# First layer's output product: its last 512 weight rows by seven block products instead of a plain product

## The chip, the cores and the metric

The kernel runs on one core of a Trainium2 chip. Times are device microseconds (us) of one launch. One execution of the kernel was also recorded by the hardware profiler. All views below are of that execution; in them times count from the start of its span.

## The reference, cut to what matters

A two-layer encoder works on 512 tokens of width 1024. The first layer mixes tokens by dilated window attention (8 heads of 128), the second by grouped-query attention with axial rotary positions. Each layer also attends over 256 memory rows (4 heads of 128), gates the twelve heads' outputs with a SiLU and multiplies them by an output matrix of 1536 x 1024. That last product, in the first layer, is what the change is about.

```python
for i in range(DEPTH):
    h = rmsnorm(x, norm_g[i])
    mem_h = rmsnorm(mem, mem_norm_g[i])
    ...
    o_mem = memory_attention(q_mem, mem_h, w_mem_kv[i], mem_qn_g[i], mem_kn_g[i])
    y = jnp.concatenate([o_mix, o_mem], axis=-1) * jax.nn.silu(gate)
    x = x + jnp.einsum('bse,ed->bsd', y, w_out[i])
return x
```

Everything is fp32.

## The kernel before, in words

**Products.** An fp32 product is made of three matmuls on operands that are split in two: a rounded copy (the high half) and what the rounding left out (the low half). `mm_early` issues high x high (line 176) and activation low x weight high (line 177), `mm_late` issues activation high x weight low (line 180). A group of twelve 512-wide matmuls is the unit of work. In the group's order all eight of lines 176 and 177 stand first, alternating, and the four of line 180 last.

**Weights.** All weights lie in one array in the order of their use. `PLAN` names the kind of each stretch, `Weights` loads pieces of 0.5 MB with SyncE's queue as buffers come free (`KEEP` sets how many may be alive), copies them to a high half on ScalarE (line 323) and subtracts for the low half on VectorE (line 333). Both halves lie in rings of four. Each group advances the ring.

**Seven products for eight.** `s_chunk` multiplies a 2 x 2 block matrix of activations by a 2 x 2 block matrix of weights with seven block products (Winograd's form of Strassen's scheme). The seven activation operands ("forms": 12, 11, S1, S2, S4, S3, 22) are sums of the four blocks, and the seven weight operands (21, 11, T1, T2, 22, T3, T4) sums of the weight blocks. T1 and T3 are loads that add to a block already loaded; T2 and T4 add one tile to another within SBUF. These adding transfers go through GpSimd's queue (lines 261 and 307; T1 of early stretches, below the index `T1_DMA`, is added by VectorE at line 297). Products that share a term are accumulated in one PSUM bank. `keep` copies a bank out after a product, `add` adds to such copies (lines 411 and 420). With `tail` given, which only the second layer's output product did, form 22 comes ahead of S3, its product in a bank of its own, and the handlers in `tail` carry the sums into the residual.

**Order.** Nothing is left to a scheduler. The program is written as coroutines that a hand-written driver steps: one slot (`drv.tick`) for each group of matmuls. `drv.release(gen, d)` starts the work behind a product after d slots, `yield n` gives up n slots, `drv.late` and `drv.soon` put an instruction at the end or the start of a slot. So the order on each engine is fixed when the program is built, and each engine runs its own in that order. A semaphore wait stops everything behind it on its engine.

**The first layer's end.** `gates` makes, for the four gate blocks of gate group g = 2 (heads 4 to 7 of the attention), the gate times the heads' outputs: line 870 writes y in fp32, line 894 copies it to a high half (ScalarE), line 896 subtracts (VectorE). Heads' outputs go through a tensor in device memory, except that of head 7 (`DIRECT`), the last one computed, which is taken from SBUF. `out_proj` first multiplies the other 1024 rows of the output matrix by `s_chunk` (two weight tiles for each of its products; `tight`, `place`), the sums going to the tiles `acc`, to each of which a transfer adds x (line 1003, GpSimd's queue). Then `out_rest` multiplies y of g = 2 by the remaining 512 rows: per half of the tokens (two blocks of 128) and per half of the columns two groups, eight in all, on two stretches "O1" of the plan with two weight tiles each. Line 806 adds each group's result to `acc`.

**What follows it.** `ev_o` takes each finished block of 128 tokens of x1, the second layer's input: it writes it to device memory (line 1459), makes the sum of squares (`norm_1`, lines 527 and 529), scales it by the norm (`norm_2`, line 534) and transposes it with TensorE (`turn4`, line 540), whose result is copied to a high half (line 164, ScalarE) and subtracted for a low half (line 167, VectorE). The first two blocks ("upper rows") end in `first_t`, the last two ("lower rows") in `diffs_t` and `rest_t`, which make the second layer's forms (lines 600, 601 and 609 among them). Meanwhile `mem_norm(1)`, started 14 slots (`MEM_B`) after line 1469, normalises the memory rows for the second layer (the tiles `m`, line 534 also), and they are transposed by lines 540, 164 and 167 as well, in the slots of the stage that is changed. Behind it come eight groups of `mem_kv`, the second layer's memory keys and values, with squares of heads on ScalarE (line 633) and multiplications on VectorE (line 638).

**The second layer's end** has the same last 512 rows already done by `s_chunk(512, YL, ..., K=2, tail=...)`: `prep_l` (line 954) makes the forms, and its `put` hands the two halves to the driver:

```python
def put(k, src):
    t = m4(F32R, "yl" + k)
    drv.late(lambda: A.copy(t[:, 0:512], src))
    drv.soon(lambda: V.tensor_tensor(t[:, 512:1024], src, t[:, 0:512].bitcast(F32), ALU.subtract))
```

Of the kernel before, what the change touches and what calls it, by code (L numbers as in the profile page):

```python
# [10 lines left out]
F32 = mybir.dt.float32  # L11
# [25 lines left out]

PLAN = ["W2"] + ["T2"] * 2 + ["W1", "W2s"] + ["W2" if c.isdigit() else "W1" for c in A_ORDER[1:]] + ["W2"] + ["O1"] * 2 + ["T2b"] * 2 + ["W1bs", "W2c"] + ["W1b"] * 4 + ["W2b", "W1o"]

SEQ = [1, 2, 0] + list(range(3, len(PLAN)))  # L40
T4_AT = {4: 4}
T1_DMA = 17
SUM_AT = {"T1": 7, "T3": 10}
# [88 lines left out]
def trunk_kernel(ctx: ExitStack, tc: tile.TileContext, x, mem, wall, norm_g, mem_norm_g, gcol,  # L132
# [257 lines left out]
    def s_chunk(n, act, ev, tokens=True, pre=None, half=False, soon=False, tight=False, place=None, pairs=False, K=4, tail=None):  # L390
# [35 lines left out]
        def mid(u, b):  # L426
            t = snap["21", u] = s2(name="sn")
            tail[1](u, t, b)
            yield 1

        if tail:
            after = after[:5] + ((mid,),)
        for i, (a, s, fresh) in enumerate(PRODUCTS[:5] + (("22", 2, True), ("S3", 1, False)) if tail else PRODUCTS):
# [4 lines left out]
            for x in range(K // per):  # L438
# [7 lines left out]

                if tail and i == 6:
                    for b, c in ((0, slice(0, 512)), (1, slice(0, 512))):
                        o, ts = bank[s][b][:, c], slice(b * 128, (b + 1) * 128)
                        for k in range(per):  # L450
                            mm_early(o, ah[:, k, ts], wh[:, k, c], al[:, k, ts], wh[:, k, c], False)
                        for k in range(per):
                            mm_late(o, ah[:, k, ts], wo[:, k, c], k == per - 1)
                        while ("21", 1) not in snap:
                            drv.free()
                            drv.tick()
                        tail[2](b, snap["21", b], snap["s5", b], o, c)
                    continue
# [373 lines left out]
    def gates(od, o_done, o_here, direct, forms=False):  # L832
# [121 lines left out]
        def prep_l():  # L954

            def put(k, src):
                t = m4(F32R, "yl" + k)
                drv.late(lambda: A.copy(t[:, 0:512], src))
                drv.soon(lambda: V.tensor_tensor(t[:, 512:1024], src, t[:, 0:512].bitcast(F32), ALU.subtract))
                YL[k] = t.rearrange("p (a k t) -> p a k t", a=2, k=2)  # L960

            while ys[2] is None:
                yield 1
            put("12", ys[2])
            yield 1
            while ys[0] is None:
                yield 1
            put("11", ys[0])
            yield 1
            while ys[1] is None or ys[3] is None:  # L970
                yield 1
            a11, a21, a12, a22 = ys
            s1, s2_ = s2(name="yl"), s2(name="yl")
            V.tensor_tensor(s1, a21, a22, ALU.subtract)
            put("S1", s1)
            yield 1
            V.tensor_tensor(s2_, s1, a11, ALU.subtract)
            put("S2", s2_)
            yield 1
            V.tensor_tensor(a12, a12, s2_, ALU.add)  # L980
            put("S4", a12)
            yield 1
            put("22", a22)
            yield 1
            V.tensor_tensor(a21, a11, a21, ALU.subtract)
            put("S3", a21)

        return gate, prep_y, YW, (prep_l, YL) if forms else ys

    def out_proj(YW, ys, src, evac, tiles, half=False, last=None):  # L990
# [15 lines left out]

        if last:
            prep_l, YL = ys
            drv.spawn(prep_l())
        s_chunk(512, YW, ev, half=half, tight=True, place=place)  # L1010
        if not last:
            out_rest(ys, acc, done, evac)
            return

        def ev_l(q, u, t):
# [6 lines left out]
        def sum_11(u, z, p):  # L1022
# [4 lines left out]
            yield 1  # L1027
            yield from evac(0, u, acc[u])

# [17 lines left out]

        s_chunk(512, YL, ev_l, tight=True, K=2, tail=(sum_kept, sum_21, final, sum_11))

# [392 lines left out]

    gate, prep_y, YW, ys = gates(od, o_done, o_here, DIRECT)
    for c in A_ORDER:
# [345 lines left out]
```

## Time and profile before

| what | value |
|---|---|
| median of 3 runs | 943.03 us (942.79 to 943.77) |
| the profiled execution's own time | 942.18 us |
| span of its profile, first to last instruction | 940.4 us |
| busy: PE / PEld / DVE / ACT / POOL | 99% / 87% / 85% / 74% / 37% |
| lines 176, 177, 180 in the chain that ended last | 25% of the span each |
| bytes moved | 207.15 MB, 220 GB/s on average |

PE is TensorE's matmul side, PEld its weight load, DVE is VectorE, ACT is ScalarE, POOL is GpSimd, SP is SyncE. A row of the list of waits reads: engine, tile, line, "<-" and the engine, tile and line that ended the wait, then its total in us, the count and the longest. A row of a timeline reads: start and duration in us, engine, line, operation, what is written "<-" what is read, the shapes, and the number of equal instructions that the row takes together; brackets behind it give the idle time ahead and what ended it. A row of the windows reads: the stretch, its length, the busy time of PE, PEld, DVE, ACT and POOL with their instructions, the granted clock of TensorE, the share of the DMA engines' time and the GB/s. A row of the DMA issues reads: what is written and read, queue, count, KB each, median us from issue to landing. Matmuls overlap, so a matmul's time in a row is longer than its distance to the next.

### The profile page before, as it was taken

What the parts mean: (1) busy time and instruction counts of PE and PEld (TensorE: products, weight loads), DVE (VectorE), ACT (ScalarE), POOL (GpSimd) and SP (SyncE); (2) the same over time, 40 slices, a digit from 0 to 9 for tenths busy, and PEclk for the clock granted to TensorE, in tenths of its full rate; (3) what the DMA queues carried; (4) which work ended last, traced back from release to release, by engine and by line L of the source; (5) the groups of instructions that cost most, each with busy time, mean ns of one, the idle gap of its engine ahead of it and who ended that gap; (6) DMA issues with size and microseconds to landing.
All of it is one profiled execution on the core that took longest, in us unless ns stands there. A gap on an engine that the chain in (4) does not pass through costs nothing.

```text
span 940.4 us, 16301 instructions
## 1 busy us (share of the span) xinstructions
PE 932.0 (99%) x5500; PEld 819.4 (87%) x5500; DVE 799.6 (85%) x1443; ACT 691.6 (74%) x1720; POOL 348.4 (37%) x494
## 2 busy tenths in 40 slices
PE   8999999999999999999999999999999999999998
PEld 6889888888888888888889998888988999999886
DVE  6998776879888888889788999877998998689978
ACT  7775788677768686867675768537878887789773
POOL 3412425455554545463836111214252440110122
PEclk9999999999999999999999999999999999999999
DMA  9999937869787878696867979979985686785777
GB/s 346 387 259 324 316 93 189 278 133 262 155 251 146 261 155 267 158 268 136 242 177 190 269 202 249 291 239 317 270 201 118 171 240 167 198 225 121 200 159 179
DMA packets 89285, 207.15 MB, mean 220 GB/s; under 512 B 25201, under 2 KB 34417, under 8 KB 89202
## 3 DMA queue, kind: packets, MB, share of 16 engines
q1 hardware_dynamic: 68674, 140.51, 43.5%
q0 software_dynamic: 19520, 63.97, 36.8%
q10 hardware_dynamic: 1008, 1.64, 0.5%
q8 instruction: 43, 0.70, 0.3%
q14 instruction: 40, 0.33, 0.1%
HBM read 158.31 MB, written 11.08 MB: 180 GB/s over the span
## 4 chain that ended last, share of the span: by engine, by line
PE 95%; DVE 2%; ACT 1%; DMA 1%; issue 0%; SPq 0%; DVEq 0%; ACTq 0%
PE pj L177 25%; PE pj L176 25%; PE pj L180 25%; PE qT L645 3%; PE sa L1305 2%; PE oo L1413 2%; PE pt L1392 1%; PE ptb L1619 1%; PE sa L1301 1%; PE xT L540 1%; PE ob L180 1%; PE ob L177 1%; PE ob L176 1%; PE sb L171 1%; PE sb L170 1%; PE sb L172 1%
## 5 line engine op out<-in xcount | busy, mean ns | idle before, releaser
L333 DVE TENSOR_TENSOR wo<-wl,wh 128x1024 fp32r<-128x1024 f32 x258 | 316.3, 1232 | 6.9 <-ACT wh L323 6.7
L323 ACT CAST wh<-wl 128x1024 fp32r<-128x1024 f32 x258 | 272.1, 1061 | 31.0 <-PE pj L177 17.4
L176 PE MATMUL pj<-wh,hS 128*128 128x512 f32 (+1 forms) x416 | 154.4, 380 | 0.0
L177 PE MATMUL pj<-wh,hS 128*128 128x512 f32 (+1 forms) x416 | 149.0, 367 | 0.0
L176 PE MATMUL pj<-wh,h 128*128 128x512 f32 (+1 forms) x312 | 115.3, 378 | 0.0
L177 PE MATMUL pj<-wh,h 128*128 128x512 f32 (+1 forms) x312 | 111.7, 367 | 0.0
L488 POOL TENSOR_TENSOR rstd<-mse,half 128x4 f32<-128x4 f32 (+2 forms) x98 | 103.4, 1056 | 8.2
L180 PE MATMUL pj<-wo,hS 128*128 128x512 f32 (+1 forms) x416 | 99.5, 366 | 0.0
L177 PEld LDWEIGHTS pj<-wh,hS 128*128 128x128 f32 x416 | 78.7, 189 | 11.2
L176 PEld LDWEIGHTS pj<-wh,hS 128*128 128x128 f32 x416 | 78.6, 189 | 11.1 <-DVE sn L420 0.2
L487 POOL TENSOR_SCALAR mse<-hss 128x4 f32<-128x4 f32 (+1 forms) x88 | 47.8, 543 | 101.9 <-ACT junk L633 94.2
L180 PEld LDWEIGHTS pj<-wo,hS 128*128 128x128 f32 x416 | 72.5, 189 | 13.1
L633 ACT ACTIVATE junk<-sn 128x128 f32<-128x128 f32 x264 | 79.4, 311 | 2.7 <-DVE sn L411 2.6
L398 ACT COPY sn<-pj 128x512 f32<-128x512 f32 x122 | 67.1, 588 | 17.8 <-PE pj L180 17.0
L1249 POOL TENSOR_TENSOR ta<-sn,tabs 128x128 f32<-128x128 f32 (+1 forms) x64 | 35.8, 566 | 119.0 <-DVE sn L638 91.8
L180 PE MATMUL pj<-wo,h 128*128 128x512 f32 (+1 forms) x312 | 74.5, 365 | 0.0
L307 POOL DMA_DIRECT2D wl<-wl x34 | 30.2, 897 | 113.3 <-DVE wo L333 73.3
L261 POOL DMA_DIRECT2D wl<-in_wall_dram x40 | 38.0, 966 | 80.4 <-DMA wl<-in_wall_dram 41.0
L177 PEld LDWEIGHTS pj<-wh,h 128*128 128x128 f32 x312 | 59.0, 189 | 8.4
L176 PEld LDWEIGHTS pj<-wh,h 128*128 128x128 f32 x312 | 59.0, 189 | 8.2
L420 DVE TENSOR_TENSOR sn<-pj,sn 128x512 f32<-128x512 f32 x89 | 60.8, 684 | 5.7 <-PE pj L180 5.3
L180 PEld LDWEIGHTS pj<-wo,h 128*128 128x128 f32 x312 | 54.3, 189 | 9.7
(290 smaller groups left out, 2367.2 us busy)
## 6 DMA issues: line engine op xcount, KB each, us to landing
wl<-in_wall_dram SPq DMA_DIRECT2D x224, 512.0 KB, 7.4
wl<-wl POOLq DMA_DIRECT2D x68, 512.0 KB, 5.5
wl<-in_wall_dram POOLq DMA_DIRECT2D x44, 512.0 KB, 8.5
od<-o SPq DMA_DIRECT2D x11, 256.0 KB, 5.4
og<-od SPq DMA_DIRECT2D x10, 256.0 KB, 9.5
x<-in_x_dram SPq DMA_DIRECT2D x4, 512.0 KB, 9.1
v0d<-sn SPq DMA_DIRECT2D x8, 256.0 KB, 8.5
acc<-in_x_dram POOLq DMA_DIRECT2D x8, 256.0 KB, 6.2
```

What stands on the lines that cost most here:

```text
L176: T.matmul(o, a, b, start=start, stop=False, skip_group_check=True)
L177: T.matmul(o, c, d, start=False, stop=False, skip_group_check=True)
L180: T.matmul(o, a, b, start=False, stop=stop, skip_group_check=True)
L261: queue.dma_start(t, wall[d], **how)
L323: A.copy(wh, self.tile[self.items[i]])
L333: V.tensor_tensor(wo, self.tile[key], wh.bitcast(F32), ALU.subtract)
L398: A.copy(t, b)
L420: V.tensor_tensor(t, b, t, ALU.subtract if q == "12" else ALU.add)
L487: G.tensor_scalar(e, ss, EPS, None, ALU.add)
L488: G.tensor_tensor(r, e, half[:, 0:n], ALU.pow)
L633: A.activation(jk, p[:, j * 128:(j + 1) * 128], AF.Square, scale=by, accum_out=ss[:, j:j + 1])
L1249: G.tensor_tensor(ta[:, 0:n], xn[:, 0:n, 0:32], ropeA[:, 0, b, s0:s0 + n], ALU.mult)
```

## The change

The last 512 weight rows of the first layer's output matrix (last in the kernel's order: those of attention heads 4 to 7, gate group g = 2) are no longer multiplied by `out_rest` but by `s_chunk` with K = 2, as in the second layer. Eight groups of twelve matmuls on four weight pieces become seven groups on seven weight tiles, which six loads and four adding steps make: T1 and T3 are loads that add (`T1_DMA` goes from 17 to 16, so that this stretch's T1 is one too), T2 and T4 adds within SBUF. `gates` in the first layer is called with `forms=True`: the high and low halves of y (lines 894 and 896) are not made; `prep_l` makes the seven forms from the fp32 y instead.

`tail` now has a fifth part, and its third may be empty. Empty, as in the first layer, the last product is issued like the others and `fin` adds its bank to the sums kept, both column halves of a lower block at once, and passes them to `ev_o`. In the second layer the last product is still done column half by column half.

`prep_l`'s `put` no longer hands its instructions to the driver: it issues the high half at once, gives up a slot and issues the low half in the next one. That holds for both layers; in the second layer each engine's order of instructions is the same as before.

```diff
-PLAN = ["W2"] + ["T2"] * 2 + ["W1", "W2s"] + ["W2" if c.isdigit() else "W1" for c in A_ORDER[1:]] + ["W2"] + ["O1"] * 2 + ["T2b"] * 2 + ["W1bs", "W2c"] + ["W1b"] * 4 + ["W2b", "W1o"]
+PLAN = ["W2"] + ["T2"] * 2 + ["W1", "W2s"] + ["W2" if c.isdigit() else "W1" for c in A_ORDER[1:]] + ["W2", "W1o"] + ["T2b"] * 2 + ["W1bs", "W2c"] + ["W1b"] * 4 + ["W2b", "W1o"]
...
-T1_DMA = 17
+T1_DMA = 16
...
+        def fin(u, b):
+            t, c = snap["21", u], snap["s5", u]
+            V.tensor_tensor(t, b, t, ALU.add)
+            V.tensor_tensor(c, c, b, ALU.subtract)
+            yield 1
+            yield from tail[4](u, t, c)
+
         if tail:
-            after = after[:5] + ((mid,),)
+            after = after[:5] + ((mid,), (fin,))
...
-                if tail and i == 6:
+                if tail and tail[2] and i == 6:
...
             def put(k, src):
                 t = m4(F32R, "yl" + k)
-                drv.late(lambda: A.copy(t[:, 0:512], src))
-                drv.soon(lambda: V.tensor_tensor(t[:, 512:1024], src, t[:, 0:512].bitcast(F32), ALU.subtract))
+                A.copy(t[:, 0:512], src)
+                yield 1
+                V.tensor_tensor(t[:, 512:1024], src, t[:, 0:512].bitcast(F32), ALU.subtract)
                 YL[k] = t.rearrange("p (a k t) -> p a k t", a=2, k=2)
...
-            put("12", ys[2])
-            yield 1
+            yield from put("12", ys[2])
...
-        if last:
-            prep_l, YL = ys
-            drv.spawn(prep_l())
+        prep_l, YL = ys
+        drv.spawn(prep_l())
         s_chunk(512, YW, ev, half=half, tight=True, place=place)
-        if not last:
-            out_rest(ys, acc, done, evac)
-            return
-
...
-            yield from evac(0, u, acc[u])
+            if last:
+                yield from evac(0, u, acc[u])
...
-        s_chunk(512, YL, ev_l, tight=True, K=2, tail=(sum_kept, sum_21, final, sum_11))
+        s_chunk(512, YL, ev_l, tight=True, K=2, tail=(sum_kept, sum_21, last and final, sum_11, lambda u, *o: evac(1, 2 + u, o)))
...
-    gate, prep_y, YW, ys = gates(od, o_done, o_here, DIRECT)
+    gate, prep_y, YW, ys = gates(od, o_done, o_here, DIRECT, True)
```

In the changed kernel the lines above 428 keep their numbers and those below move by a few: 527, 529, 534, 540, 638 and 870 become 534, 536, 541, 547, 645 and 877. The rows of order below, of the changed kernel, have its own numbers. Line 967 is `put`'s subtraction, lines 980, 982, 984 and 987 make the forms S1, S2, S4 and S3.

The first place is VectorE's order in the stage itself. `wo` are weights' low halves, `m` the memory rows, `act` their low halves after the transposes, `pj` banks of PSUM, `yl` and `sn` tiles of 512 columns. Before:

```order
L896 TENSOR_TENSOR y_6824<-sn_7042,y_6823 128x2x256
L896 TENSOR_TENSOR y_6824<-sn_7002,y_6823 128x2x256
L420 TENSOR_TENSOR acc_7339<-pj_7498,acc_7339 128x512
L420 TENSOR_TENSOR acc_7340<-pj_7499,acc_7340 128x512
L333 TENSOR_TENSOR wo_7535<-wl_7410,wh_7534 128x1024
L806 TENSOR_TENSOR acc_7217<-pj_7557,acc_7217 128x512
L333 TENSOR_TENSOR wo_7574<-wl_7443,wh_7573 128x1024
L534 SCALAR_TENSOR_TENSOR m_7545<-m_7545,rm_73,row_7543 128x512 x2
L806 TENSOR_TENSOR acc_7218<-pj_7578,acc_7218 128x512
L534 SCALAR_TENSOR_TENSOR m_7546<-m_7546,rm_73,row_7543 128x512 x2
L167 TENSOR_TENSOR act_7617<-xT_7619,act_7615 128x4x128
L167 TENSOR_TENSOR act_7618<-xT_7626,act_7616 128x4x128
```

And now, from the first scaling of the memory rows on:

```order
L541 SCALAR_TENSOR_TENSOR m_7539<-m_7539,rm_73,row_7537 128x512 x2
L967 TENSOR_TENSOR ylS1_7578<-yl_7575,ylS1_7578 128x512
L982 TENSOR_TENSOR yl_7576<-yl_7575,sn_6892 128x512
L333 TENSOR_TENSOR wo_7600<-wl_7438,wh_7599 128x1024
L541 SCALAR_TENSOR_TENSOR m_7540<-m_7540,rm_73,row_7537 128x512 x2
L167 TENSOR_TENSOR act_7640<-xT_7642,act_7638 128x4x128
L167 TENSOR_TENSOR act_7641<-xT_7649,act_7639 128x4x128
L967 TENSOR_TENSOR ylS2_7608<-yl_7576,ylS2_7608 128x512
L984 TENSOR_TENSOR sn_7038<-sn_7038,yl_7576 128x512
L333 TENSOR_TENSOR wo_7632<-wl_7298,wh_7631 128x1024
L167 TENSOR_TENSOR act_7640<-xT_7684,act_7638 128x4x128
L167 TENSOR_TENSOR act_7641<-xT_7691,act_7639 128x4x128
```

The additions of a group's result (line 806) are gone. The scalings of the memory rows and their low halves (lines 541 and 167) stand where they stood in the stage, and the forms and their low halves (lines 982, 984 and 967) stand between them: S2's low half right behind the first pair of lines 167, S4's behind the second pair.

The second place is TensorE around the fourth of the seven groups, the product of form S2, now:

```order
L177 MATMUL pj_7612<-wh_7528,ylS1_7578 128x512
L176 MATMUL pj_7613<-wh_7528,ylS1_7578 128x512
L177 MATMUL pj_7613<-wh_7528,ylS1_7578 128x512
L180 MATMUL pj_7612<-wo_7529,ylS1_7578 128x512 x2
L180 MATMUL pj_7613<-wo_7529,ylS1_7578 128x512 x2
L547 MATMUL xT_7642<-ident_68,m_7539 128x128 x4
L547 MATMUL xT_7649<-ident_68,m_7539 128x128 x4
L176 MATMUL pj_7580<-wh_7569,ylS2_7608 128x512
L177 MATMUL pj_7580<-wh_7569,ylS2_7608 128x512
```

The eight transposes that the first pair of lines 167 reads (`xT`) stand directly ahead of the group, and its second matmul (line 177) reads the low half that VectorE makes behind that pair. The transposes themselves have not moved: before, too, they stood behind the third and the fourth group of the stage.

The third place is VectorE where the lower rows of x1 are scaled for the second layer, during the groups of `mem_kv`. Before:

```order
L167 TENSOR_TENSOR h12_7800<-xT_7853,h12_7800 128x4x128
L167 TENSOR_TENSOR h11_7808<-xT_7860,h11_7808 128x4x128
L333 TENSOR_TENSOR wo_7848<-wl_7576,wh_7847 128x1024
L333 TENSOR_TENSOR wo_7851<-wl_7593,wh_7850 128x1024
L534 SCALAR_TENSOR_TENSOR acc_7339<-acc_7339,rstd_7830,row_7132 128x512 x2
L534 SCALAR_TENSOR_TENSOR acc_7340<-acc_7340,rstd_7881,row_7132 128x512 x2
```

And now:

```order
L167 TENSOR_TENSOR h12_7900<-xT_7966,h12_7900 128x4x128
L167 TENSOR_TENSOR h11_7908<-xT_7973,h11_7908 128x4x128
L541 SCALAR_TENSOR_TENSOR sn_7796<-sn_7796,rstd_7878,row_7127 128x512
L541 SCALAR_TENSOR_TENSOR sn_7674<-sn_7674,rstd_7878,row_7127 128x512
L645 TENSOR_TENSOR xn_7999<-pj_7816,rstd_7955 128x512
L333 TENSOR_TENSOR wo_7961<-wl_7765,wh_7960 128x1024
L333 TENSOR_TENSOR wo_7964<-wl_7802,wh_7963 128x1024
L541 SCALAR_TENSOR_TENSOR sn_7829<-sn_7829,rstd_7930,row_7127 128x512
L541 SCALAR_TENSOR_TENSOR sn_7676<-sn_7676,rstd_7930,row_7127 128x512
```

The second scaling of the lower rows has moved behind one head's multiplication and two weights' low halves. On TensorE the upper rows' transposes stood after the first and the second group of `mem_kv` and now stand after the third and the fourth; the lower rows' stood after the fifth and the sixth and now after the sixth and the seventh.

More of the change, by code (lines that the diff above doesn't have):

```diff
@@ L963, in prep_l @@
                 yield 1
-            put("12", ys[2])
-            yield 1
+            yield from put("12", ys[2])
             while ys[0] is None:
                 yield 1
-            put("11", ys[0])
-            yield 1
+            yield from put("11", ys[0])
             while ys[1] is None or ys[3] is None:
@@ L974, in prep_l @@
             V.tensor_tensor(s1, a21, a22, ALU.subtract)
-            put("S1", s1)
-            yield 1
+            yield from put("S1", s1)
             V.tensor_tensor(s2_, s1, a11, ALU.subtract)
-            put("S2", s2_)
-            yield 1
+            yield from put("S2", s2_)
             V.tensor_tensor(a12, a12, s2_, ALU.add)
[L981 to L984, printed above, removed]
+            yield from put("S4", a12)
+            yield from put("22", a22)
             V.tensor_tensor(a21, a11, a21, ALU.subtract)
-            put("S3", a21)
+            yield from put("S3", a21)
         return gate, prep_y, YW, (prep_l, YL) if forms else ys
```

## The prediction

> **What bounds the kernel now.** I read the page's busy times first, then the list of waits of TensorE, then the timelines of TensorE, VectorE and ScalarE around the stage that is changed.
>
> ```profile
> span 940.4 us, 16301 instructions
> PE 932.0 (99%) x5500; PEld 819.4 (87%) x5500; DVE 799.6 (85%) x1443; ACT 691.6 (74%) x1720; POOL 348.4 (37%) x494
> ...
> PE row L1121 <- DMA row<-in_mem_norm_g_dram: 2.2, 1, 2.2
> PE pmt L772 <- DVE pmT L778: 0.7, 1, 0.7
> ```
>
> TensorE (PE) works through the whole span; behind its first wait of 2.2 us no wait is longer than 0.7 us. So a matmul that goes shortens the kernel by its place in the stream, and any new wait of TensorE lengthens it in full. VectorE (DVE), at 85%, is the next engine. I call the eight groups that go G1 to G8, the seven new products P1 to P7, and the eight groups of the second layer's memory keys and values that follow M1 to M8.
>
> ```profile
> 607.25 0.39 PE L176 MATMUL pj<-wh,y 128*128 128x512 f32 x1
> 609.97 0.39 PE L176 MATMUL pj<-wh,y 128*128 128x512 f32 x1
> ...
> 615.41 1.03 PE L540 MATMUL xT<-ident,m 128*128 128x128 f32 x8
> 616.20 0.48 PE L176 MATMUL pj<-wh,y 128*128 128x512 f32 x1
> 616.52 0.40 PE L177 MATMUL pj<-wo,y 128*128 128x512 f32 x1
> ...
> 630.79 0.39 PE L176 MATMUL pj<-wh,act 128*128 128x512 f32 x1
> ```
>
> G1 starts at 607.25, G2 at 609.97, M1 at 630.79. A group of 12 matmuls takes 2.72 us (0.227 each, though a row says 0.39: they overlap). Eight transposes cost 0.79 and slow the next start by about 0.10, so 0.89; 8 x 2.72 + 2 x 0.89 = 23.54 is just 630.79 - 607.25. The stage has no gap.
>
> **The matmuls that go.** Eight groups become seven: **-2.72 us**. Without any wait M1 would start at 628.07. Everything else in the change is on other engines, and costs only what TensorE waits for.
>
> **When VectorE reaches the new work.** Each product uses the low half of its form in its second matmul (line 177), not at the end of a group, so the subtraction at line 967 must be over 0.23 us after the product's start. Its place in VectorE's order stands in the section on the change.
>
> ```profile
> 603.60 1.23 DVE L333 TENSOR_TENSOR wo<-wl,wh 128x1024 fp32r<-128x1024 f32 x1 [1.71 <-ACT wh L323]
> 604.75 0.42 DVE L870 TENSOR_TENSOR sn<-sn,og 128x256 f32<-128x256 f32 x1
> 605.75 0.42 DVE L870 TENSOR_TENSOR sn<-sn,o 128x256 f32<-128x256 f32 x1
> 606.09 1.28 DVE L411 TENSOR_TENSOR acc<-acc 128x512 f32<-128x512 f32 x2
> 607.29 1.29 DVE L896 TENSOR_TENSOR y<-sn,y 128x512 fp32r<-128x512 f32 x2
> 608.50 1.28 DVE L420 TENSOR_TENSOR acc<-pj,acc 128x512 f32<-128x512 f32 x2
> 609.70 1.22 DVE L333 TENSOR_TENSOR wo<-wl,wh 128x1024 fp32r<-128x1024 f32 x1
> 612.56 1.41 DVE L534 SCALAR_TENSOR_TENSOR m<-m,rm,row 128x512 f32<-128x512 f32 x2
> ```
>
> Head 7's multiplications (line 870) are over only at 606.1, 1.2 us before the stage starts, and all forms descend from them. Nothing ahead of them moves, so they stand at 604.75 afterwards too. Back to back a 512-wide operation takes 0.60 us (606.09 to 607.29 for two; 0.69 to its own end), so each has 0.09 of overlap; less that, a weights' low part is 1.14 (1.23) and a scaled one some 0.67 (half of 1.41). From line 411 to the last form's low part the new order has 23, 6 and 4 of these: 13.8 + 6.8 + 2.7 = 23.3 us, so that one ends at 629.5 with no wait at all. P7's second matmul is due at 607.25 + 6 x 2.72 + 1.78 + 0.23 = 625.6. By VectorE's work alone, then, the stage ends 4 us late. The engine's spare time before (0.4 to 2 us here and there) is what the two fewer lines 896, eight lines 806 and TensorE's longer stage had left.
>
> ```profile
> 605.53 1.29 ACT L894 CAST y<-sn 128x512 fp32r<-128x512 f32 x2 [0.66 <-DVE sn L870]
> 616.05 1.08 ACT L164 CAST act<-xT 128x512 fp32r<-128x512 f32 x2 [8.27 <-PE xT L540]
> 616.66 1.29 DVE L167 TENSOR_TENSOR act<-xT,act 128x512 fp32r<-128x512 f32 x2 [0.77 <-ACT act L164]
> 12.64 0.68 DVE L167 TENSOR_TENSOR act<-xT,act 128x512 fp32r<-128x512 f32 x1
> 13.38 0.50 PE L177 MATMUL pj<-wh,act 128*128 128x512 f32 x1 [0.32 <-DVE act L167]
> ```
>
> The last two rows, from the program's start, are a low part that ends at 13.32 and the matmul that waits for it, 0.06 later; I use that for every release. Row by row:
>
> P1: the high half is copied where line 894 stood, over at 606.2. The low part starts at 607.29, ends at 607.98, the matmul goes at 608.04 instead of 607.48: **0.56**. P2: two lines 420 and a weights' part, low part to 610.92, matmul at 610.98 instead of 610.76: **0.22**. P3: the S1 form, a weights' part, two scalings of the memory rows, low part to 614.59, matmul at 614.65 instead of 613.70: **0.95**.
>
> P4 is a loop. Ahead of its low part VectorE's order has the two lines 167, which need ScalarE's copies of the transposes that TensorE does right before P4. From the start of those transposes (615.41 before) the second line 167 ends 2.54 later (617.95), the low part 0.60 after it, the matmul 0.06 after that: 3.20, where it would have come after 0.79 + 0.31 = 1.10. **2.10**, and the same for P5, whose low part stands behind the lines 167 of the second transposes: **2.10**. This does not depend on how loaded VectorE is. P6's low part is 1 us early. P7: from P5's low part on, 3 weights' parts and 8 others put the last one at 632.46, matmul at 632.52 instead of 631.49: **1.03**. Together 6.96, and M1 starts at 635.0, 4.2 after before's 630.79.
>
> For these waits the lower bound is the two loops alone, 4.2 (the rest would go if VectorE were 2 to 3 us ahead, and 4.0 is also its work alone). I take the walk, since its durations all stand in rows.
>
> **The second layer's low parts.** Nothing moves there: line for line the engines' orders are those of before, so the moved put costs 0. The same stage there shows what it needs to be hidden:
>
> ```profile
> 906.32 1.43 DVE L870 TENSOR_TENSOR sn<-sn,o 128x256 f32<-128x256 f32 x4
> 910.53 0.68 DVE L959 TENSOR_TENSOR yl<-sn,yl 128x512 fp32r<-128x512 f32 x1
> 928.46 0.68 DVE L959 TENSOR_TENSOR ylS<-sn,ylS 128x512 fp32r<-128x512 f32 x1
> ...
> 916.40 0.39 PE L176 MATMUL pj<-wh,yl 128*128 128x512 f32 x1
> 932.86 0.39 PE L176 MATMUL pj<-wh,ylS 128*128 128x512 f32 x1
> ```
>
> There the multiplications start 10.1 us before the first product and the low parts are 5.2 (first) and 3.7 us (last) early. In the first layer they start 2.5 us before it, 7.6 us later by that clock, and the memory rows' work comes on top.
>
> **What is late next.** x1's upper rows are now transposed after M3 and M4 instead of M1 and M2, the lower ones after M6 and M7 instead of M5 and M6: three groups apart, not four.
>
> ```profile
> 633.52 1.03 PE L540 MATMUL xT<-ident,acc 128*128 128x128 f32 x8
> 646.18 1.03 PE L540 MATMUL xT<-ident,acc 128*128 128x128 f32 x8
> 649.80 1.03 PE L540 MATMUL xT<-ident,acc 128*128 128x128 f32 x8
> ...
> 640.31 1.29 DVE L167 TENSOR_TENSOR h<-xT,h 128x512 fp32r<-128x512 f32 x2 [4.25 <-ACT h L164]
> 643.79 1.41 DVE L534 SCALAR_TENSOR_TENSOR acc<-acc,rstd,row 128x512 f32<-128x512 f32 x2
> 645.65 1.42 DVE L534 SCALAR_TENSOR_TENSOR acc<-acc,rstd,row 128x512 f32<-128x512 f32 x2 [0.46 <-POOL rstd L488]
> ```
>
> Before, the first lower block was normalised at 645.20, 11.7 us after the first transposes began, and was due at 646.18, 12.7 after: 1.0 to spare. One group less leaves it 1.7 late, if the chain (high copies, first copies, squares, weights' copies, then the second pair) is as long; the new order has the squares of four heads ahead and two weights' parts fewer, about even. **1.7**. The second block stands, in the new order, behind one head product and two weights' parts: 0.6 + 2.3 + 1.3 + 0.1 = 4.3 after the first, where TensorE takes 0.89 + 2.72 = 3.6: **0.6**. Bounds: nothing, if the chain shortens by 2.3, and 4 if it lengthens as much. For the second layer's forms behind M8 I add 0.
>
> **Weights and queues.** Four loads become six loads, two loads that add and two adds within SBUF: 3 MB more at 0.5 MB each; and four adds of 0.25 MB carry P1 and P2 into acc, on POOL's queue.
>
> ```profile
> 564.10:607.20 43.10, 43.10 (x214) 36.41 (x213) 40.12 (x63) 31.93 (x52) 6.09 (x7) 1.00 1.00 285
> ...
> wl<-wl POOLq DMA_DIRECT2D x68, 512.0 KB, 5.5
> wl<-in_wall_dram POOLq DMA_DIRECT2D x44, 512.0 KB, 8.5
> ```
>
> The rings are full there already (share 1.00, 285 GB/s): 3 MB are 10.5 us of traffic. T1's add and T2's add follow each other (8.5 + 5.5 us), POOL stands still for the first, and the x adds queue behind it; ScalarE wants T2 at about 606.7. Up to 610.4 a late landing costs nothing, since VectorE takes that tile at 611.4; later it costs one for one. I take 0, bound +3. On SP, x1's rows go out behind P5 to P7 and hold the next weights back some 4 us of a lead of over 15: 0.
>
> **Sum.** -2.72 + 6.96 + 2.3 = **+6.5 us**. The profiled execution took 942.18 (span 940.4 and 1.8 around it), so 948.7; the runs' median, 943.03, lies 0.85 above it: **949.6**.
>
> **Rivals.**
>
> *Hidden* (4%): VectorE gets to the forms 4 us earlier and the loops close, so only the matmuls count: 943.03 - 2.72 = 940.3, faster. For it: the second layer's tail. Against it: line 870 at 604.75, and a loop that starts with transposes no order can hurry. It decides from the point where P4's low part ends before P4's start.
>
> *Loops alone* (14%): P1 to P3 and P7 and the normalisations do not wait: -2.72 + 4.20 = +1.5, 944.5. Against it: 23.3 us of work in the 19.4 from 606.09.
>
> *Late weights* (12%): T2 lands behind 610.4 by 3 us, VectorE stands, all behind it slips: 952.6.
>
> *A slower clock* (5%): TensorE idles 2.1 of 5.6 us twice.
>
> ```profile
> 8.30 0.63 PE L176 MATMUL pj<-wh,act 128*128 128x512 f32 x1
> 14.18 0.39 PE L176 MATMUL pj<-wh,act 128*128 128x512 f32 x1
> ...
> core 0: 940.4 us, clock 1.000
> ```
>
> At the program's start a matmul takes 0.63, later 0.39. If P5 and P6 ran at half pace, 5.4 us more: 955. Against it: a granted clock of 1.000 over the whole span, its short waits included. The Trainium skill (TensorE: Matmul & The Clock Gate, "HAM oscillation — how this bites in real kernels") puts the limit at idle gaps of some 3.4 us. By that rule gaps of 2.1 keep the clock.
>
> The change not doing what it says would leave 96 matmuls; the order shows 84.
>
> **How the numbers follow.** The sum has 65%, the rivals 35%. Below 0.2% (1.9 us), about what a measurement of this kernel can tell from no change, lies *Hidden* on the fast side, and half of *Loops alone* could read as same. The rows I can quote make the waits, so: faster 0.04, same 0.05, slower 0.91. The range runs from the two loops and P7 alone, 944.5 + 1.0 = 945.5, to late weights, 953.
>
> **What would show it.** Right: TensorE waits on line 967 in five products, about 2.1 us each in P4 and P5; M1 near 635; VectorE without a gap from 604 to 629 but for the two loops; two waits on line 541 after M6 and M7; granted clock 1.00. Wrong: P4 and P5 without a wait, a DMA as the releaser of line 323, or a lower clock.

## The result, and the profile after

The changed kernel takes 955.93 us (median of 6 runs, 952.84 to 958.64), the kernel before 943.31 (6 runs, 942.79 to 943.97): a ratio of 1.0133, interval 1.0109 to 1.0157. It is slower by 12.6 us. The forecast was slower, 949.6 in a range of 945.5 to 953.0, so the sign was right and the size about half of what came.

The profiled execution took 958.00, its span is 956.2. The page's head:

```profile
span 956.2 us, 16326 instructions
PE 937.0 (98%) x5488; PEld 821.7 (86%) x5488; DVE 809.5 (85%) x1457; ACT 701.0 (73%) x1734; POOL 354.3 (37%) x502
```

TensorE's rows of the list of waits, without three that stood there before (lines 1119, 779 and 652):

```profile
PE pj L177 <- DVE ylS L967: 5.3, 3, 2.9
PE pj L176 <- DVE sn L420: 2.6, 1, 2.6
...
PE xT L547 <- ACT junk L640: 1.2, 1, 1.2
...
PE pj L177 <- DVE hS L616: 0.7, 1, 0.7
PE pt L1390 <- DVE p L1377: 0.7, 2, 0.5
PE pj L177 <- DVE yl L967: 0.4, 1, 0.4
PE xT L547 <- DVE sn L541: 0.4, 1, 0.4
```

Before, no wait behind the program's start was longer than 0.7. Now 6 us lie on the forms' low halves (line 967) and 5 behind the stage. Without line 1390, which lies ahead of the stage (at 540 us), the waits sum to 10.6; 12 matmuls fewer take 2.7 away; that makes 8, where the span grew by 15.8. The timeline of TensorE in the stage shows a second cost:

```profile
609.49 0.50 PE L177 MATMUL pj<-wh,yl 128*128 128x512 f32 x1 [0.40 <-DVE yl L967]
...
616.09 0.50 PE L177 MATMUL pj<-wh,ylS 128*128 128x512 f32 x1 [0.65 <-DVE ylS L967]
...
618.73 1.03 PE L547 MATMUL xT<-ident,m 128*128 128x128 f32 x8
619.52 0.48 PE L176 MATMUL pj<-wh,ylS 128*128 128x512 f32 x1
622.88 0.50 PE L177 MATMUL pj<-wh,ylS 128*128 128x512 f32 x1 [2.88 <-DVE ylS L967]
...
624.35 0.63 PE L177 MATMUL pj<-wh,ylS 128*128 128x512 f32 x1
624.78 1.91 PE L180 MATMUL pj<-wo,ylS 128*128 128x512 f32 x4
626.49 1.65 PE L547 MATMUL xT<-ident,m 128*128 128x128 f32 x8
627.90 0.48 PE L176 MATMUL pj<-wh,ylS 128*128 128x512 f32 x1
630.14 0.50 PE L177 MATMUL pj<-wh,ylS 128*128 128x512 f32 x1 [1.77 <-DVE ylS L967]
```

P4 and P5 wait for the low halves of S2 and S4, as forecast. But from 624.35 on a matmul takes 0.63 instead of 0.39, and four of line 180 take 1.91 where they took 1.07: TensorE runs at half speed. The windows give the granted clock (the column behind POOL):

```profile
615.00:620.00 5.00, 4.35 (x22) 3.10 (x21) 4.10 (x6) 2.76 (x5) 2.98 (x4) 1.00 1.08 209
620.00:625.00 5.00, 2.12 (x8) 1.79 (x9) 3.63 (x5) 2.88 (x6) 0.00 (x0) 0.93 1.07 298
625.00:630.00 5.00, 3.37 (x13) 2.58 (x12) 1.80 (x3) 3.47 (x7) 0.86 (x1) 0.73 0.65 119
630.00:635.00 5.00, 4.86 (x14) 3.85 (x15) 4.97 (x9) 2.44 (x5) 0.86 (x1) 0.66 0.75 157
```

A clock of 0.93, 0.73 and 0.66 over 5 us each is at most 0.35 + 1.35 + 1.70 = 3.4 us of TensorE's time. In the trace's record of the clock these are two stretches of 3.41 us at half clock, from 624.33 and from 631.16, and a third follows at 678.94, behind the longest wait of the second layer's first products:

```profile
679.00 0.58 PE L176 MATMUL pj<-wh,hS 128*128 128x256 f32 x1 [2.65 <-DVE sn L420]
```

So the executions differ: with a granted clock of 0.998 or 1.000 over the span they took 952.84, 953.97 and 954.44, with 0.994 to 0.996 they took 957.42, 958.00 and 958.64.

The table places the loss by four points of TensorE's timeline: P1's first matmul (607.25 before), M1 (630.79), the second layer's first product (656.13), and the transposes of line 772 in the second layer's memory attention (716.57). Each entry is how much longer the stretch up to that point is than in the profile of before.

| kernel | to P1 | stage | M1 to M8 | second layer's first products | rest | span |
|---|---|---|---|---|---|---|
| changed | 1.45 | 7.58 | 1.97 | 5.00 | -0.21 | 15.8 |
| low halves as before | -0.29 | 3.10 | 2.31 | 5.04 | -0.18 | 10.0 |
| memory rows early | 2.25 | -0.34 | 4.67 | 5.03 | -0.16 | 11.5 |
| T1 by VectorE | 0.02 | 5.36 | 2.32 | 3.60 | -0.15 | 11.2 |
| fin at once | 1.79 | 6.76 | 0.00 | 3.64 | -0.21 | 12.0 |
| three edits | 0.16 | 4.56 | 0.15 | 1.11 | -0.20 | 5.8 |
| GpSimd adds | 2.40 | -0.85 | 6.37 | 5.16 | -0.18 | 12.9 |
| no low halves | 0.20 | 2.01 | 5.34 | 4.95 | -0.14 | 12.4 |
| four edits | 2.78 | -0.79 | 0.00 | 2.55 | -0.19 | 4.4 |
| no low halves, fin at once | 1.03 | -0.09 | 1.92 | 2.57 | -0.15 | 5.3 |
| four edits, chain earlier | 4.12 | -0.56 | 5.51 | 4.28 | -0.21 | 13.1 |

Where the memory rows are early, their 1.78 us of transposes have moved from the second column to the first. In the two kernels of four edits 1.2 of the first column is P1's own wait. The rest of it need not be the change's: the profile of the first probe below, which differs from the kernel before in nothing ahead of P1, lost 2.2 there as well.

### The profile page after: what moved, and what is told of

Read it like the earlier page. It is cut to its first block, busy times and chain, and to the rows that moved or that the text cites. A ratio compares the mean times of both kernels' runs of the same rounds, so it can differ in the third digit from the quotient of the medians.

```text
span 956.2 us, 16326 instructions
## 1 busy us (share of the span) xinstructions
PE 937.0 (98%) x5488; PEld 821.7 (86%) x5488; DVE 809.5 (85%) x1457; ACT 701.0 (73%) x1734; POOL 354.3 (37%) x502
## 4 chain that ended last, share of the span: by engine, by line
PE 83%; DMA 7%; DVE 6%; ACT 3%; issue 1%; SPq 0%; DVEq 0%; POOLq 0%; ACTq 0%
PE pj L177 21%; PE pj L176 21%; PE pj L180 21%; DMA wl<-in_wall_dram 3%; PE qT L652 2%; DVE wo L333 2%; DMA wl<-wl 2%; DMA og<-od 1%; PE ptb L1617 1%; PE sa L1303 1%; PE oo L1411 1%; PE sa L1299 1%; PE pt L1390 1%; PE xT L547 1%; PE ob L180 1%
## 5 line engine op out<-in xcount | busy, mean ns | idle before, releaser
L333 DVE TENSOR_TENSOR wo<-wl,wh 128x1024 fp32r<-128x1024 f32 x261 | 320.3, 1232 | 7.0 <-ACT wh L323 6.8
L323 ACT CAST wh<-wl 128x1024 fp32r<-128x1024 f32 x261 | 275.4, 1060 | 32.1 <-PE pj L177 18.3
L176 PEld LDWEIGHTS pj<-wh,hS 128*128 128x128 f32 x416 | 79.7, 192 | 13.8 <-DVE sn L420 2.9
L177 PEld LDWEIGHTS pj<-wh,hS 128*128 128x128 f32 x416 | 79.8, 192 | 12.2 <-DVE hS L616 0.9
L180 PEld LDWEIGHTS pj<-wo,hS 128*128 128x128 f32 x416 | 72.4, 189 | 13.1
L398 ACT COPY sn<-pj 128x512 f32<-128x512 f32 x128 | 70.4, 590 | 16.8 <-PE pj L180 15.9
L261 POOL DMA_DIRECT2D wl<-in_wall_dram x42 | 40.2, 973 | 93.8 <-DMA wl<-in_wall_dram 33.6
L307 POOL DMA_DIRECT2D wl<-wl x35 | 31.0, 896 | 117.1 <-DVE wo L333 72.1
L297 POOL DMA_DIRECT2D wl<-wl x35 | 32.9, 976 | 84.2 <-DVE wl L292 18.7
```

Source lines behind the costliest of these rows:

```text
L176: T.matmul(o, a, b, start=start, stop=False, skip_group_check=True)
L177: T.matmul(o, c, d, start=False, stop=False, skip_group_check=True)
L180: T.matmul(o, a, b, start=False, stop=stop, skip_group_check=True)
L261: queue.dma_start(t, wall[d], **how)
L323: A.copy(wh, self.tile[self.items[i]])
L333: V.tensor_tensor(wo, self.tile[key], wh.bitcast(F32), ALU.subtract)
```

## The experiments

**Low halves as before.** One part of the change is undone: `put` hands its halves to the driver.

```diff
-                A.copy(t[:, 0:512], src)
+                drv.late(lambda: A.copy(t[:, 0:512], src))
+                drv.soon(lambda: V.tensor_tensor(t[:, 512:1024], src, t[:, 0:512].bitcast(F32), ALU.subtract))
                 yield 1
-                V.tensor_tensor(t[:, 512:1024], src, t[:, 0:512].bitcast(F32), ALU.subtract)
```

> The changed kernel with the forms' low halves handed to the driver as before (high half at a slot's end, low half at the next slot's start), nothing else. S2's and S4's low halves then stand ahead of the memory rows' low halves on VectorE. Theory A (the two loops through the memory rows' transposes, and the half-speed stretches of TensorE's clock that follow their long waits): the wait in P4 goes to 0, that in P5 to under 1 us, no stretch at half speed in the stage, 949 us. Rival B (late weights: the adding transfers hold ScalarE, and VectorE behind it): the waits shrink by under 1 us each and the time stays at 954 or above. Rival C (most of it arises behind the stage, at the second layer's forms): the stage gains, the end does not, 953.

952.60 (951.68 to 954.14), ratio 1.0110 (1.0096 to 1.0124). TensorE's waits:

```profile
PE pj L176 <- DVE sn L420: 2.6, 1, 2.6
...
PE pj L177 <- DVE ylS L966: 1.9, 1, 1.9
PE xT L547 <- ACT junk L640: 1.5, 1, 1.5
PE at L177 <- DVE yl L966: 1.4, 1, 1.4
```

P4's and P5's waits are gone and no stretch of the stage is at half speed: the stage lost 3.1 instead of 7.6. What came in their place is late VectorE: 1.4 at P6, behind the second pair of lines 167, and 1.9 at P7. So the place of the low halves cost about half of the stage's loss. The time fell by only 3 (2.2 by the ratios), since the 5 us at the second layer's first products stayed (5.00 and 5.04). That was Rival C's point, and no theory of the stage explains it.

**Memory rows early** (`MEM_B` 6 for 14).

> The changed kernel with the memory rows' loads, scalings, transposes and low halves 8 slots earlier (MEM_B 6 for 14), ahead of the last multiplications of y. Theory A: no loop is left; VectorE's 5 us of memory work fall into a stretch where it idles 2.6 us, so the forms start about 2.4 us later, one wait of 2.5 to 3 us at P1 or spread over P1 to P3, none in P4 and P5: 949 us, 951 if the wait at P1 brings a stretch at half speed. Rival B: three loads more in a stretch whose queues are full make the weights later still: 956 or more. Rival C: 953.

953.20 (952.68 to 953.62), ratio 1.0113 (1.0097 to 1.0128). P4 and P5 no longer wait, P1 waits 1.3, and P7 waits 1.6, which theory A did not have. The stage's -0.34 holds the 1.78 of the moved transposes, so without them it is 1.4 longer than before, with one group less. Part of what the stage gained is lost behind it: M1 to M8 lost 4.67. Theory A was right on P4 and P5 and 4 us too fast on the whole.

**T1 by VectorE** (`T1_DMA` 17 for 16).

> The changed kernel with T1 of this stretch made by VectorE (T1_DMA 17 for 16): one adding transfer less on GpSimd's queue, one 1024-wide addition more on VectorE. Theory A: T4 may land early enough that ScalarE's copies of the transposes are on time (0.9 us less in P4), and VectorE has 1.2 us more to do: 955 us, within 1.5 of the changed kernel. Rival B: the adding transfers are the cause, and the time falls to 951 or below.

954.72 (953.04 to 959.19), ratio 1.0134 (1.0114 to 1.0154), where the changed kernel has 1.0133: no gain, so Rival B falls. But the profile separates a term. In the changed kernel ScalarE's timeline shows T4 arriving late, ahead of the copies that the first pair of lines 167 needs, and VectorE's shows what that delays:

```profile
619.38 1.05 ACT L323 CAST wh<-wl 128x1024 fp32r<-128x1024 f32 x1 [1.11 <-DMA wl<-wl]
620.33 1.07 ACT L164 CAST act<-xT 128x512 fp32r<-128x512 f32 x2
```

```profile
620.94 1.29 DVE L167 TENSOR_TENSOR act<-xT,act 128x512 fp32r<-128x512 f32 x2 [1.84 <-ACT act L164]
622.15 0.68 DVE L967 TENSOR_TENSOR ylS<-yl,ylS 128x512 fp32r<-128x512 f32 x1
```

With T1 by VectorE the two loops stand bare in TensorE's timeline:

```profile
617.29 1.03 PE L547 MATMUL xT<-ident,m 128*128 128x128 f32 x8
...
620.48 0.50 PE L177 MATMUL pj<-wh,ylS 128*128 128x512 f32 x1 [1.93 <-DVE ylS L967]
...
623.12 1.03 PE L547 MATMUL xT<-ident,m 128*128 128x128 f32 x8
...
626.31 0.71 PE L177 MATMUL pj<-wh,ylS 128*128 128x512 f32 x1 [1.92 <-DVE ylS L967]
```

From the transposes' start to the second matmul: 620.48 - 617.29 = 3.19 and 626.31 - 623.12 = 3.19, where the forecast had 3.20 and a wait of 2.10. In the changed kernel P4's was 3.05: 0.95 of it is the late T4.

**The clock, probe one.** The kernel before, with five operations that change nothing ahead of the last two lines 896:

```diff
+                if len(y_done) == 10:
+                    for _ in range(5):
+                        V.tensor_tensor(t, t, t, ALU.max)
```

> The kernel before with five 512-wide operations that change nothing (a maximum of y with itself) ahead of the last two subtractions of line 896: 3.0 us more on VectorE, so that TensorE waits once, for about 2.6 us, at the first group's line 180, and all else is as before. If a wait costs its length alone: 943.2 + 2.6 = 945.8 in every execution, granted clock 1.000. If a wait of 2 to 3 us is followed by a stretch at half speed: 1.7 us more, 947.5, with a clock below 1.000 in those executions that show it.

945.31 (945.02 to 948.32), ratio 1.0038 (1.0025 to 1.0050). Four executions took 945.02 to 946.10, one 948.32. The profile is of that one:

```profile
613.90 0.94 PE L180 MATMUL pj<-wh,y 128*128 128x512 f32 x2 [1.99 <-DVE y L899]
614.64 0.63 PE L176 MATMUL pj<-wh,y 128*128 128x512 f32 x1
```

One wait of 2.0 us is followed by half speed, in the kernel before, with nothing of the change in it. The other four took 2.7 to 3.8 more than the kernel before, at a clock of 0.999 that the kernel before shows too, so with no such stretch of their own. How long they waited was not recorded.

**The clock, probe two** (eight operations for five).

> The kernel before with eight 512-wide operations that change nothing ahead of the last two subtractions of line 896: 4.8 us on VectorE, one wait of TensorE of about 4.2 us. If a stretch at half speed follows when most of one of the clock's 3.4 us stretches was idle (as in the one of five executions with the shorter wait that took 948.3 us), every execution shows it here: 942.3 + 4.2 + 1.7 = 948.2. If it came by chance: 946.5 in most.

949.20 (948.47 to 949.46, 6 runs), ratio 1.0070 (1.0058 to 1.0082), clock 0.996 or 0.997 in every one.

```profile
614.15 1.22 PE L180 MATMUL pj<-wh,y 128*128 128x512 f32 x2 [4.18 <-DVE y L899]
```

A wait of 4.2 us costs 6.8, each time. In the profile two stretches of 3.41 us at half speed follow each other, from 612.23 to 619.06; the first begins during the wait, and beside the wait 2.6 us are lost.

**fin at once** (its `yield 1` is left out).

> The changed kernel, but fin passes the lower rows on in the slot in which it sums them (its yield 1 is gone), so that their squares, their scaling and their transposes come one group earlier on every engine, where they were before the change. The product stage is not touched. Theory D (the eighth group that went was also the time in which the lower rows' chain of squares, norm and transposes ran, so behind the stage 2.6 + 0.7 us of waits and a stretch at half speed are lost at the second layer's forms): those waits go to under 1 us, the waits at the lower rows' transposes grow by 1 to 2, and the time falls by 2 to 4, to 951 to 953. Rival E (the chain itself is as long as its engines' work and only its place moves): the waits move to the transposes in full, and the time stays at 954 to 956.

952.35 (949.10 to 954.48), ratio 1.0097 (1.0077 to 1.0116): 3.6 less than the changed kernel. M1 to M8 lose 0.00 instead of 1.97, and of the second layer's waits 1.94 of 3.34 is left:

```profile
PE pj L177 <- DVE ylS L966: 5.8, 4, 2.3
...
PE pj L176 <- DVE sn L420: 1.9, 1, 1.9
```

The time is theory D's, and rival E's 954 to 956 did not come. The split is another than D had: the waits at the transposes, which were to grow by 1 to 2, are gone, and of the waits behind, which were to fall under 1, more than half is left.

**Three edits:** low halves as before, T1 by VectorE, fin at once.

> Three edits at once: the low halves handed to the driver as before, T1 by VectorE, and fin without its yield. Theory D with A: in the stage the waits of the first experiment (about 3.1 us behind the kernel before at the stage's end, less up to 1 for T4), behind it 2 to 4 less: 948 us. Rival E: 951 to 952.

948.56 (947.94 to 951.05), ratio 1.0070 (1.0057 to 1.0083), where Theory D with A had 948. The sum came out, its parts did not: the stage lost 4.56, 1.5 more than in the first experiment, with a stretch at half speed from 632.35, and behind it M1 to M8 and the first products lost 6.1 less than there, not 2 to 4.

**GpSimd adds:** low halves as before, memory rows early, fin at once, and lines 1016 and 1034 on GpSimd in the first layer.

> The low halves handed to the driver, the memory rows 8 slots earlier, fin without its yield, and the four additions to the residual of lines 1016 and 1034 on GpSimd instead of VectorE. If VectorE's amount of work in the stage is what is left of the loss (theory A's second part), the wait at P7 goes and the stage ends about 1 us behind the kernel before: with theory D 946 to 948 us. If GpSimd's own queue (its adding transfers) now holds these sums, the waits come back at the lower rows' transposes: 950 to 952. Faster than the kernel before, under 942.3, is not expected of any theory.

954.52 (952.86 to 957.36), ratio 1.0131 (1.0116 to 1.0146): a miss, more than 6 us above the forecast. GpSimd's timeline, then ScalarE's (in this kernel and those below, lines stand one lower or up to three higher, as their edits shift them):

```profile
633.78 1.57 POOL L1015 TENSOR_TENSOR acc<-sn,acc 128x512 f32<-128x512 f32 x1
```

```profile
635.39 0.63 ACT L533 ACTIVATE sq<-acc 128x512 f32<-128x512 f32 x1 [1.79 <-POOL acc L1015]
...
636.01 1.03 ACT L323 CAST wh<-wl 128x1024 fp32r<-128x1024 f32 x1
```

The two additions of this line take 1.57 and 2.10 there, where VectorE's took 0.69. The square behind it holds ScalarE, the weights' copy for M1 stands behind the square, and M1 waits 3.69, long enough for half speed.

**No low halves.** The forms' low halves are left out in the first layer: ScalarE writes a second copy in their place.

```diff
                 A.copy(t[:, 0:512], src)
+                if direct is DIRECT:
+                    A.copy(t[:, 512:1024], src)
                 yield 1
-                V.tensor_tensor(t[:, 512:1024], src, t[:, 0:512].bitcast(F32), ALU.subtract)
+                if direct is not DIRECT:
+                    V.tensor_tensor(t[:, 512:1024], src, t[:, 0:512].bitcast(F32), ALU.subtract)
```

> The changed kernel with the subtraction for the forms' low halves left out in the first layer: a second copy by ScalarE stands in the low half's place, so the numbers of the product are not the reference's. Seven 512-wide operations less on VectorE, and no low half stands behind lines 541 or 167 any more. Theory A: P1 to P5 do not wait, TensorE reaches the memory keys' groups up to 2.7 us earlier than in the kernel before, and no stretch at half speed falls in the stage. Theory D: what that gains comes back behind the stage, since the lower rows' chain is not shorter: waits at their transposes and at the second layer's forms of 5 to 8 us, and 945 to 949 in all. If D is wrong and all came from the stage: 941 to 943.

952.57 (950.05 to 954.58), ratio 1.0103 (1.0085 to 1.0121): no better than moving them. One wait in the stage is left, and it is not for a form:

```profile
PE pj L176 <- ACT sn L398: 2.8, 1, 2.8
PE pj L176 <- DVE sn L420: 2.6, 1, 2.6
```

The S4 form itself (line 984) stands behind the first pair of lines 167 too, ScalarE waits for it with its high half, and the copy of the bank that P5 needs (line 398) stands behind that. So the loop does not need a low half, and this wait too was followed by a stretch at half speed (from 624.16), which theory A had excluded. Behind the stage 10 us are lost. That the loss moves there is as D says; its 5 to 8 us, and its 945 to 949, were too little.

**Four edits:** the three, and the memory rows 6 slots earlier.

> The low halves handed to the driver, T1 by VectorE, fin without its yield, and the memory rows 6 slots earlier (MEM_B 8 for 14). Against the same three edits without the last (948.6): theory A says the loop that is left (P6's low half behind the second pair of lines 167, 1.4 us) goes and P7's wait shrinks, 945 to 947. If the earlier memory rows only push y's multiplications later by their 5 us of VectorE: 948 to 950.

948.25 (946.52 to 949.71), ratio 1.0057 (1.0044 to 1.0070). P6 and P7 no longer wait, M1 to M8 lose nothing. y's multiplications are later instead, as the second case had it, and P1 waits for its form's high and low half (lines 964 and 965):

```profile
PE pj L176 <- DVE sn L420: 1.9, 1, 1.9
PE pj L177 <- DVE yl L965: 1.7, 1, 1.7
PE pj L176 <- ACT yl L964: 1.2, 1, 1.2
```

**No low halves, fin at once.**

> As the kernel without the low halves' subtraction (the same part of the computation left out), and fin without its yield. Theory D: the waits behind the stage shrink by 2 to 4 us, and this, with most of the forms' work taken away, is the first to come near the kernel before: 942 to 945. If TensorE's matmuls alone bounded the rest, one group less would show in full: 939.7.

948.56 (947.45 to 949.77), ratio 1.0066 (1.0051 to 1.0081). Even with seven operations of VectorE left out, the kernel is 6 us slower than before; expected were 942 to 945. In its profile no stretch but the last is at half speed, and the span is still 5.3 longer.

**Four edits, chain earlier:** the scaling of the lower rows one slot earlier still (`EO[0] - (b >= 2)`).

> The kernel of the four edits (948.3), with the lower rows' scaling and transposes one group earlier once more (the wait between norm_1 and norm_2 one slot shorter for them). Theory D: the 1.9 us wait at the second layer's forms and the half-speed stretches behind it go, at the price of up to 1 us at the transposes: 945.5 to 947. Rival E: TensorE waits at the transposes instead, by as much: 948 to 949. Not under the kernel before (942.4) by either.

953.93 (953.73 to 955.32), ratio 1.0124 (1.0107 to 1.0140): 5.7 worse. TensorE's waits:

```profile
PE xT L546 <- ACT f L597: 3.4, 1, 3.4
...
PE pj L176 <- DVE sn L420: 2.0, 1, 2.0
```

Neither theory had this time, and the 3.4 us are not the longer chain of rival E. VectorE's and ScalarE's timelines show where they begin:

```profile
645.59 1.42 DVE L540 SCALAR_TENSOR_TENSOR sn<-sn,rstd,row 128x512 f32<-128x512 f32 x2 [2.97 <-DMA x1d<-sn]
```

```profile
649.90 1.18 ACT L597 COPY f<-xT 128x512 f32<-128x512 f32 x2 [5.68 <-DVE h L167]
```

The scaling, a slot earlier, now waits 2.97 us until the transfer that writes the unscaled block of x1 to device memory has read it. The upper rows' low halves (line 167) stand behind it on VectorE, ScalarE's copies behind these, and the lower rows' transposes wait for the copies. The wait at the second layer's first products is still 2.0, so the place of the scaling alone does not decide that one. No version came under the kernel before.

## Why the prediction was right and wrong

- *The matmuls.* 96 became 84 and nothing else of TensorE's work changed: 5500 to 5488 in the page. Right.
- *P1 to P3.* Forecast 0.56, 0.22, 0.95; measured 0.56 (609.49 for 608.93), 0.07 and 0.81. Right.
- *P4 and P5.* Forecast 2.10 each, "does not depend on how loaded VectorE is". Measured 3.05 and 1.93, and 2.09 and 2.10 with T1 by VectorE. The loop was right. Late weights, put at 0 with a bound of +3, were looked for at T2 alone. T2 cost nothing: ScalarE waits 3.08 for it, until 611.21, and VectorE takes it at 612.89 without a wait. T4 added 0.95, and on ScalarE, not through VectorE's weights' part.
- *P7.* Forecast 1.03, measured 0: from P5's second matmul to P7's, two groups, TensorE took 7.2 us in place of 5.4, 3.4 of them at half speed, and VectorE had its time. (The 632.46 of the forecast follows from 2 weights' parts and 7 others behind P5's low part, which is what stands there, not from the 3 and 8 that its sentence counts.) The waits of the stage come to 6.42 in all, forecast 6.96.
- *x1's rows.* Forecast 2.3 for M1 to M8, measured 1.97, and 2.31 and 2.32 in two experiments that leave this part alone. Right for the changed kernel (with *memory rows early* and *no low halves* it was 4.67 and 5.34), though for the first block the row names ScalarE's head squares (line 640), not the scaling.
- *"For the second layer's forms behind M8 I add 0".* This step failed. Two waits there came to 2.65 + 0.69, with a half-speed stretch behind the first: 5.0 us. The prediction had counted how the lower rows' scaling falls behind when the stage is one group shorter, and stopped at TensorE's next use of it. The forms behind it had lost the same group. The trace of before shows that there was nothing to spare: the product that now waits 2.65 started 0.06 after line 420's end.

```profile
664.56 0.68 DVE L420 TENSOR_TENSOR sn<-pj,sn 128x512 f32<-128x512 f32 x1
```

```profile
665.30 0.39 PE L176 MATMUL pj<-wh,hS 128*128 128x256 f32 x1
```

And now, on VectorE:

```profile
671.38 0.69 DVE L167 TENSOR_TENSOR hS<-fS,hS 128x512 fp32r<-128x512 f32 x1 [1.42 <-ACT hS L164]
...
677.65 0.69 DVE L616 TENSOR_TENSOR hS<-f,hS 128x512 fp32r<-128x512 f32 x1 [0.90 <-ACT hS L615]
678.26 0.68 DVE L420 TENSOR_TENSOR sn<-pj,sn 128x512 f32<-128x512 f32 x1
```

Counted from the second layer's first product (656.13 before, 667.12 now), line 420 ends 11.82 us later in place of 9.11: 2.7. VectorE's stretch of work up to it, from the second head's multiplication (line 645, before 638) on, starts 3.88 us ahead of that product in place of 4.93, and takes 15.70 us in place of 14.04, since it waits 1.42 and 0.90 for ScalarE's high halves of the forms. In *four edits* the same stretch takes 14.07 us and waits for nothing, but it starts only 2.41 us ahead of the product, 2.5 less than before, behind a wait of 1.62 for that head's norm from GpSimd (line 494). That accounts for the 1.9 that is left there, and is near the 2.72 of the group that went; why the norm comes late was not tested.
- *The clock.* "By that rule gaps of 2.1 keep the clock"; the slower clock was a rival with 5%. This failed too: 3.4 us at most in the stage of the profiled execution, 1.7 at most behind it, nothing in the quickest executions. The quickest execution, 952.84 at a granted clock of 1.000, is still 3.2 us above the sum, about the two waits of the missing term (3.34); it left no trace, so this is not shown.
- *Against the chances.* The sum had 65% and was too small; the rival *Slower clock* named the right mechanism at P4 and P5, and its reason against was wrong. That its 955 came close to 955.9 is luck: half speed cost 3.4 us at most in the stage where it had 5.4, and it did not have the 5.0 behind M8.

What the change gives back is now plain: one group less on TensorE is 2.72 us, and the chain that runs beside it (forms, sums, norm, transposes, the second layer's forms on VectorE and ScalarE) did not get shorter but longer (15.70 us for 14.04 in its last stretch). Where that chain meets TensorE the 2.72 was lost again: *fin at once* shows it for the transposes, and for line 420 in part.

## What to carry to other kernels

When a bound engine loses work, list every later meeting with the chain that runs beside it, not the next one only: each had its slack in that work. In an order fixed by hand, look for loops, where an operation waits behind another engine's answer to work that stands just ahead of its own user; moving it a slot was worth 2 to 3 us here. Price a wait of TensorE of about 2 us at its length plus up to 1.7, and a longer one higher: that of 4.2 us cost 2.6 more.

## What the runs showed of the hardware that was not expected

Half speed comes in stretches of 3.41 us on a grid that runs through, and follows a stretch in which TensorE was idle for a little more than half. Over all 14 profiles, with the waits added up within each such stretch, the program's start and end left out: 1.84 us idle or more (19 stretches), and the next one was at half speed every time; 1.68 or less (23 with more than 0.8), never; of three between 1.77 and 1.81, once. So the same wait of 2 us costs 2 or 3.7 as it falls on the grid. That fits the first probe's 945 to 946 four times and 948 once, and the changed kernel's spread over 5.8 us where the kernel before spreads over 1.2; only one execution of each kernel was recorded. The Trainium skill (TensorE: Matmul & The Clock Gate, "What's actually happening") has the free-running window of 3413 ns, and these runs agree with it (3.41 us); that the window must be idle is not what they show, 1.84 of 3.41 us were enough.
